# Two threads for the inverses, an urgent rank for what the column products lack, two-copy grams and recounted times in a hand-ordered encoder kernel

## The chip, the cores and the metric

The kernel runs on one core of a Trainium2 chip. The metric is the device time of one execution in microseconds. Inside the core, TensorE (PE) multiplies matrices into PSUM, VectorE (DVE) and ScalarE (ACT) do elementwise work and bring results out of PSUM, GpSimd (POOL) and SyncE (SP) mostly issue DMAs. Each engine works through its own instructions strictly in order and waits at semaphores for the others.

## The reference

Two requests of 512 tokens with 1024 features pass the same two layers. Layer 0 is RWKV-7 time mixing in both directions, layer 1 a neighbourhood attention on a grid of 8 x 64 tokens.

```python
def _wkv7_scan(r, decay, k, v, a, b, reverse):
    def step(s, inp):
        r_t, w_t, k_t, v_t, a_t, b_t = inp
        sa = jnp.einsum('bhvk,bhk->bhv', s, a_t)
        s = s * w_t[:, :, None, :] + sa[..., None] * b_t[:, :, None, :] + v_t[..., None] * k_t[:, :, None, :]
        return s, jnp.einsum('bhvk,bhk->bhv', s, r_t)
...
    for d in range(2):
        w_log = -jax.nn.softplus(-(w0[d] + jnp.tanh(xw @ w1[d]) @ w2[d]).astype(f32)) - 0.5
        decay = heads(jnp.exp(-jnp.exp(w_log)))
        a = heads(jax.nn.sigmoid((a0[d] + (xa @ a1[d]) @ a2[d]).astype(f32)))
        k_d = k * (1.0 + (a - 1.0) * k_a_h)
        ys.append(_wkv7_scan(r, decay, k_d, v, -kk, kk * a, reverse=(d == 1)))
```

Around this stand the large products with weights of 1024 columns each (`w_r`, `w_k`, `w_v`, `w_z`, `w_o`; then `w_in` with 4096 columns and `w_ao`), all in float32.

## The kernel before

**Stages.** The first stage (`prelude`) normalises the inputs and makes the first products. The second, `scan_phase`, holds the whole recurrence of both requests and, between its pieces, the large products that do not hang on it. The third, `rest`, holds the attention and the last products. A large product of float32 is made of three matmuls on rounded halves (high by high, high by low, low by high), so each weight tile must first be split: ACT writes the high half `whi` (line 782), DVE the low half `wlo` (line 784). The input tiles are split in the same way into pairs of `act` tiles (lines 808 and 810).

**The scan.** Tokens are cut into 8 chunks of 64. The 16 heads go in pairs of pairs, so that 2 requests x 4 give 8 *pairs*, each with 8 *steps*: 64 steps in a row. `prep` (twice for each pair) builds the scaled keys and queries (`ab`), and `gram` multiplies them into 32 x 32 blocks on PE (line 1012); ACT brings these from PSUM into `Gd` and `Go` (lines 1018 and 1019). `inverse` inverts the unit lower triangles: it transposes `Gd` into `N` on DVE (line 1048), makes 30 rank-1 updates there (lines 1055 and 1057, the *elimination*), writes the result transposed as `NA` and `MT` (lines 1065 and 1070), and then joins blocks of 32 into blocks of 64 by small matmuls and copies (lines 1074 to 1096, the *merges*). A step (`step`, `near`, `outer`, `factors`) solves with `MT` (matmuls of line 1250) and carries the state `S` on.

**What sets the order.** In `scan_phase` the order of PE, DVE and ACT is written by hand. Every piece of work is a `Thread`, a generator that yields before each instruction that has something to wait for. `weave` asks all threads whose gate is open and takes, among those that are ready by the counted time, the one with the lowest rank: steps 0, near and factors 0.5, outer 1, prep 1.5, the posts of columns (what follows a product) 2, operands 2.5, splits 3 where the stock is low and else 9, the inverse 5, the column products 9. The class `Clock` counts the times: it adds a cost for each instruction to the time of its engine. Only this counted time decides the order; on the chip the semaphores decide when a thing runs. Where nothing is ready for PE in the counted time, `weave` puts in a *filler* matmul (line 1681) that multiplies constants into an unused part of PSUM, as long as PE was busy for less than 70% of the last 3.4 us.

**Gates.** The inverse of pair n starts when its prep is through, when the inverse before it is through (it is one thread) and when the steps of the pair before the last are done. Prep n+1 starts when elimination n has taken `Gd`. Products of a group of columns (one input, such as `lv` of request 1) go in order: each column takes 8 input tiles k, and each k three matmuls (lines 863, 864, 865). Their gate asks for `w` (the split weight), `x` (the split input), a PSUM bank and, at k = 0, for the post of the column before the last.

Of the kernel before, what the change touches and what calls it, by code (L numbers as in the profile page):

```python
# [50 lines left out]
class Clock:  # L51
# [7 lines left out]
    def __init__(self, nc):  # L59
        self.nc = nc  # L60
        self.t = dict.fromkeys("PADGS", 0.0)
        self.made, self.used = {}, {}
        self.slots = {}
        self.slot = {}
        self.keep = set()
        self.dq = 0.0
        self.mode, self.tiles = None, {}
        self.seen = 0
        self.work = []
# [43 lines left out]
    def one(self, e, i):  # L113
# [51 lines left out]
        return 0.0 if e in "SG" and "dram" in str(type(outs[0].bass_ap.tensor)).lower() else done  # L165

    def matmul(self, i, ins, n, t):
        f32, tr = ins[0].dtype == F32, bool(i.is_transpose)
# [63 lines left out]
class Trunk:  # L232
# [21 lines left out]
    HACT = (3, 4)  # L254
    WARM = 300.0
    AHEADE = dict(S=3000.0, A=200.0, D=200.0)

# [85 lines left out]
    def consts(self):  # L343
# [17 lines left out]
        ts = nc.vector.tensor_scalar  # L361
        ts(dv[:, 0:32], v("w0", 32), 0.5, None, op0=ALU.mult)
        ts(dv[:, 32:40], v("ka", 8), 0.5, None, op0=ALU.mult)
        ts(dv[:, 40:48], v("ka", 8), -0.5, 1.0, op0=ALU.mult, op1=ALU.add)
# [303 lines left out]
    def column(self, s, kind, p, ps):  # L668
# [29 lines left out]
        if kind == "k":  # L698
# [15 lines left out]
            if p == NP - 1:  # L714
# [6 lines left out]
                yield "D"  # L721
                vt.tensor_scalar(rn, rn, 1e-12, None, op0=ALU.max)
                vt.reciprocal(rn, rn)
# [34 lines left out]
    def flow(self):  # L758
# [124 lines left out]

    def prep(self, s, p):
# [34 lines left out]
        vt.tensor_tensor(w2l, w2, w2h.bitcast(F32), op=ALU.subtract)  # L919
        yield "A", None, need(kk)  # L920
        km = b("km")
        act.mul(km, kk, -0.5)
        kps = []
        grams = None
        free, room = self.bank()
        for d in range(2):
            ths = []
            for q, bias in ((d, 8 * d + p), (2 + d, 16 + 8 * d + p)):
# [7 lines left out]
                th = b(f"th{q // 2}")  # L936
                act.activation(th, ps, AF.Tanh, scale=0.5, bias=self.dv[:, bias:bias + 1])
                ths.append(th)
                if len(ths) == 1:
                    u = b("u")  # L940
                    act.activation(u, th, AF.Identity, bias=self.one)
            if grams:
# [36 lines left out]
            yield "D", None, need(tha)  # L979
            vt.scalar_tensor_tensor(bb, tha, 1.0, kk, op0=ALU.add, op1=ALU.mult)  # L980
            yield "D", None, lambda c: max(need(e1)(c), ck)
            put(3, mul, c3(r), e1v)
            yield "D"
            put(2, mul, c3(km), e0v)
            yield "D", None, need(e2)
# [12 lines left out]
            def gram(ab=ab, d=d):  # L998
# [16 lines left out]
                yield "A", None, need(ps)  # L1015
                for par in range(2):
                    e = (par + d) % 2
                    act.copy(Gd[half(e), :, par::2, g], ps[half(e), :, :, 0:32])
                    act.copy(Go[half(e), :, par::2, g], ps[half(e), :, :, 32:64])

# [14 lines left out]

    def inverse(self, s, pb):

# [4 lines left out]
        NU = 32  # L1042
        free, room = self.bank()
        need = lambda *xs: lambda c, n=[x.tensor.name for x in xs]: c.at(n)
# [21 lines left out]
        MT = self.MTb[self.nM % 2]  # L1066
        self.nM += 1

        yield "D"
        vt.transpose(MT[:, :, 0, :].rearrange("p u i -> p i u"), N)  # L1070
        yield "A"
        for q in (1, 3):
# [123 lines left out]
    def step(self, q):  # L1196
# [49 lines left out]
        def solved():  # L1246
            for g in range(2):
                for h in range(2):
                    for r in range(2):
                        nc.tensor.matmul(  # L1250
                            u[half(1 - r), h, g], mt[half(r), h, st.i, g], Z[half(r), h, g], start=True, stop=True)
                        yield
# [443 lines left out]
    def scan_phase(self, mid):  # L1696
# [6 lines left out]
        self.MTb = [t(f"MT{j}", (P, 32, 2, 32)) for j in range(2)]  # L1703
        self.nM = 0

        self.cab = [t(f"cab{j}", (P, 17 * L)) for j in range(2)]
# [51 lines left out]
        def each(f):  # L1758
# [5 lines left out]
            Thread(lambda: 1, each(self.outer)),  # L1764
            Thread(lambda: 0, fetch()), Thread(lambda: 0, fetch_x()), *self.flow(), Thread(lambda: 5, inverse()), Thread(lambda: 1.5, preps()),
            Thread(lambda: 1.3 if did["finish"] == 3 else 4, finish()), Thread(lambda: 1.2, self.norm0(0))]
# [203 lines left out]
```

## Time and profile before

| quantity | value |
|---|---|
| median of 3 runs | 1650.11 us (1646.97 to 1652.83) |
| profiled execution | 1650.23 us |
| its span, first to last instruction | 1648.5 us |
| matmul passes of PE in the span | 18784 |
| filler matmuls (line 1681) | 80, of two passes each |

The span is what the profile's views divide. The first stage ends at about 150 us, the stage with the scan at about 1160 us. A float32 matmul whose operands are not rounded halves runs in two or four passes, so PE's counts in the profile are higher than in the program. A row of the groups view gives the line, engine and operation, the tiles (output before the arrow, inputs behind), the shape, the count, the union of busy time in us, the mean of one in ns and, behind the second bar, the idle time of the engine just before these instructions and what ended it.

### The profile page before, as it was taken

The page shows a single profiled execution, that of the slowest core. Times are in us where ns is not written, and L with a number is a line of the kernel's source. Part 1 is how long each engine was busy: PE and PEld are TensorE (multiplying, and loading weights), DVE is VectorE, ACT ScalarE, POOL GpSimd, SP SyncE. Part 2 cuts the span into 40 slices and gives each one's busy share as a digit, 9 for nine tenths or more (in the row PEclk, how much of TensorE's full clock was granted, in tenths as well). Part 3 has the DMA queues.
Part 4 walks back from the last instruction along what each step waited for, and adds up shares of the span by engine and source line. Part 5 has one row for each costly group of instructions (what it writes and reads, how often), then busy time and mean ns, then how long its engine had stood idle before and what let it go on. Part 6 is the DMA issues. An engine that isn't in the chain of part 4 may idle for free.

```text
span 1648.5 us, 46529 instructions
## 1 busy us (share of the span) xinstructions
PE 1545.7 (94%) x18784; PEld 1184.1 (72%) x18784; DVE 1218.2 (74%) x2713; ACT 1012.6 (61%) x2027; POOL 178.8 (11%) x336
## 2 busy tenths in 40 slices
PE   7988999889998999988989899999999999999998
PEld 5866767666676776766767667777777778777776
DVE  8986587678788797877898887855676585665564
ACT  6567676757765667667666655453667665465562
POOL 0001123201011011231010110000000002100000
PEclk9989999899999999999999999999999999999999
DMA  6447686766668578777687664564865346745553
GB/s 239 160 169 258 202 272 219 250 227 229 194 197 267 189 237 278 225 251 242 219 273 222 215 228 148 169 193 144 285 222 167 104 141 215 245 156 175 169 165 104
DMA packets 182008, 340.48 MB, mean 207 GB/s; under 512 B 25344, under 2 KB 58240, under 8 KB 181792
## 3 DMA queue, kind: packets, MB, share of 16 engines
q1 hardware_dynamic: 158144, 256.75, 48.4%
q0 software_dynamic: 23648, 80.76, 13.9%
q8 instruction: 148, 2.42, 0.6%
q14 instruction: 68, 0.56, 0.1%
HBM read 230.33 MB, written 107.09 MB: 205 GB/s over the span
## 4 chain that ended last, share of the span: by engine, by line
PE 45%; DVE 3%; ACT 3%; DMA 2%; issue 1%; DVEq 0%; POOL 0%; ACTq 0%; SPq 0%; POOLq 0%
PE pg L430 6%; PE pg L431 6%; PE pg L432 6%; PE pm L863 3%; PE pm L865 3%; PE pm L864 3%; PE sc L1489 2%; PE po L1522 2%; PE pt L1507 2%; PE pf L1151 1%; PE us L1250 1%; PE us L1270 1%; PE zy L1223 1%; PE pm L1476 1%; PE zy L1274 1%
## 5 line engine op out<-in xcount | busy, mean ns | idle before, releaser
L863 PE MATMUL pm<-act,whi 128*128 128x512 f32 x672 | 297.3, 442 | 2.9 <-ACT whi L782 2.2
L865 PE MATMUL pm<-act,wlo 128*128 128x512 f32 x672 | 268.7, 400 | 11.4 <-DVE wlo L784 10.7
L864 PE MATMUL pm<-act,whi 128*128 128x512 f32 x672 | 267.4, 398 | 6.9 <-DVE act L810 6.9
L865 PEld LDWEIGHTS pm<-act,wlo 128*128 128x128 f32 x672 | 127.9, 190 | 47.5 <-DVE wlo L784 18.4
L863 PEld LDWEIGHTS pm<-act,whi 128*128 128x128 f32 x672 | 127.7, 190 | 44.8 <-issue 12.9
L430 PE MATMUL pg<-act,whi 128*128 128x512 f32 x384 | 159.6, 416 | 0.0
L431 PE MATMUL pg<-act,whi 128*128 128x512 f32 x384 | 152.4, 397 | 0.0
L432 PE MATMUL pg<-act,wlo 128*128 128x512 f32 x384 | 152.1, 396 | 0.0
L864 PEld LDWEIGHTS pm<-act,whi 128*128 128x128 f32 x672 | 128.6, 191 | 31.9 <-DVE act L810 10.5
L379 ACT CAST whi<-raw 128x512 fp32r<-128x512 f32 x148 | 91.4, 617 | 85.5 <-PE pg L431 61.7
L784 DVE TENSOR_TENSOR wlo<-raw,whi 128x512 fp32r<-128x512 f32 x168 | 114.0, 683 | 39.8 <-ACT whi L782 39.5
L380 DVE TENSOR_TENSOR wlo<-raw,whi 128x512 fp32r<-128x512 f32 x148 | 101.3, 686 | 55.1 <-ACT whi L379 54.7
L782 ACT CAST whi<-raw 128x512 fp32r<-128x512 f32 x168 | 102.7, 618 | 43.2 <-PE pm L864 32.9
L432 PEld LDWEIGHTS pg<-act,wlo 128*128 128x128 f32 x384 | 72.1, 188 | 15.0 <-issue 0.3
L430 PEld LDWEIGHTS pg<-act,whi 128*128 128x128 f32 x384 | 72.3, 188 | 14.7 <-issue 3.3
L431 PEld LDWEIGHTS pg<-act,whi 128*128 128x128 f32 x384 | 72.5, 189 | 13.6 <-issue 2.5
L1057 DVE TENSOR_TENSOR N<-etmp,N 128x30 f32<-128x30 f32 (+14 forms) x240 | 78.7, 328 | 4.5
L1055 DVE TENSOR_TENSOR etmp<-N 128x30 f32<-128x30 f32 (+14 forms) x240 | 78.4, 327 | 4.2
L1151 PE MATMUL pf<-cab 64*64 64x128 f32 (+1 forms) x2048 | 68.5, 270 | 6.5 <-issue 6.5
L1500 DVE CUSTOM_DVE_ANT_0 sb<-sc,bias 128x256 f32<-128x256 f32 x128 | 49.6, 419 | 27.5 <-PE pt L1507 17.3
L1503 ACT ACTIVATE sb<-sb,mx 128x256 f32<-128x256 f32 x128 | 64.2, 503 | 9.3 <-DVE mx L1502 8.5
L1174 DVE TENSOR_TENSOR AK<-zy,cc 128x256 f32<-128x256 f32 x63 | 26.6, 422 | 56.4 <-PE zy L1129 53.0
(391 smaller groups left out, 3598.1 us busy)
## 6 DMA issues: line engine op xcount, KB each, us to landing
dab<-ab POOLq DMA_DIRECT2D x32, 1024.0 KB, 6.8
cab<-dab SPq DMA_DIRECT2D x64, 512.0 KB
raw<-in_w_in_dram SPq DMA_DIRECT2D x128, 256.0 KB
bias<-in_rpb_dram SPq DMA_DIRECT2D x32, 384.0 KB
raw<-in_w_z_dram SPq DMA_DIRECT2D x32, 256.0 KB
raw<-in_w_k_dram SPq DMA_DIRECT2D x32, 256.0 KB
raw<-in_w_r_dram SPq DMA_DIRECT2D x32, 256.0 KB
k<-dk SPq DMA_DIRECT2D x32, 256.0 KB
```

Of the source, the lines that this page charges most:

```text
L379: self.nc.scalar.copy(hi, src)
L380: (eng or self.nc.vector).tensor_tensor(lo, src, hi.bitcast(F32), op=ALU.subtract)
L430: nc.tensor.matmul(ps, hi, x[k][0], start=(k == 0), stop=False)
L431: nc.tensor.matmul(ps, hi, x[k][1], start=False, stop=False)
L432: self.mm = nc.tensor.matmul(ps, lo, x[k][0], start=False, stop=(k == KT - 1))
L782: nc.scalar.copy(hi, raw[h])
L784: nc.vector.tensor_tensor(lo, raw.pop(h), hi.bitcast(F32), op=ALU.subtract)
L863: nc.tensor.matmul(ps, hi[:, at], xh, start=(k == 0), stop=False)
L864: nc.tensor.matmul(ps, hi[:, at], xl, start=False, stop=False)
L865: nc.tensor.matmul(ps, lo[:, at], xh, start=False, stop=(k == KT - 1))
L1057: vt.tensor_tensor(N[:, q + 1:, :q], tv, N[:, q + 1:, :q], op=ALU.add)
L1151: end = nc.tensor.matmul(st.f[half(a), h, 0, d, g] if st.last else st.f[half(a), h, :, d, g], ab[half(h), d, g, 2 * e[d] + 1 - a], rt if s ...
```

## The change

Six things are altered.

1. `inverse` becomes two threads: `elimination` (rank 5) and `merges` (rank 2.4). Elimination n no longer waits for the merges of n-1 and for the steps of pair n-2 before it starts, only before it writes `NA` and `MT`.
2. The threads that supply products get the rank 1.2 while theirs is the first thing lacking within the next 8 input tiles of the column products: `short()` says whether that is a split weight, a split input or a post.
3. The grams leave PSUM in two ACT copies of 128 partitions instead of four of 64. The blocks then stand in another order, which the index of `mt` in `step` takes up.
4. The factor -0.5 that `km` (line 922) carried goes elsewhere: `rn` is scaled by the root of 2, `tha` is computed with a negative sign, and `dv` has other constants. The ACT instruction for `km` goes, and `kk` takes its place.
5. `u` is made by a copy with the number 1.0 instead of an activation with a tile of ones as bias.
6. `Clock` counts other times: 46 ns instead of 85 as ACT's start for an input in PSUM, 105 ns for each further operand of ACT, 112 ns where ACT changes its rows, 1283 ns for a change of its function table, 1.13 ns for each element of a DVE operation with a scalar and two tensors, and 104 and 48 ns on PE between matmuls on the full array and on parts of it.

The chains of work outside `scan_phase` are the same instructions.

```diff
@@ Clock.one
             if e == "A":
-                c = 85.0 + 0.85 * n
+                c = self.scalar(i, ins, outs, n)
...
-                c = 82.0 + 1.02 * n
+                c = 82.0 + (1.13 if getattr(i, "is_scalar_tensor_tensor", False) else 1.02) * n
@@ Clock
+    def scalar(self, i, ins, outs, n):
+        ap = outs[0].bass_ap
+        rows = (ap.offset // ap.ap[0][0] if ap.ap[0][0] else 0, ap.ap[0][1])
+        c = (46.0 if ins[0].bass_ap.tensor.name.startswith(self.BANKS) else 85.0) + 0.85 * n + 105.0 * (len(ins) - 1)
+        if rows != (0, 128) and rows != self.rows or self.rows[1] < 128 and rows[1] == 128:
+            c += 112.0
...
+            if self.table is not None and (f == "Sqrt") != self.table:
+                c += 1283.0
@@ Clock.matmul
+        full = ts == (128, 128)
+        if full and not tr and self.mode not in (None, ts):
+            c += 104.0
+        elif not full and self.mode == (128, 128):
+            t += 48.0
@@ Trunk
+    AHEADB, URGENT = 8, 1.2
@@ flow
+        def short():
+            for n in range(self.AHEADB):
+                b = did["k"] + n
+                c, k = divmod(b, KT)
+                if c >= len(cols):
+                    return None, n
+                if b // 4 not in w:
+                    return "w", n
+                if (cols[c][0], k) not in x:
+                    return "x", n
+                if k == 0 and c - 2 in self.post:
+                    return "post", n
+            return None, n
+        def rank(kind, usual):
+            def now():
+                what, n = short()
+                return self.URGENT if what == kind else usual()
+            return now
...
-            Thread(lambda: 0, loads()), Thread(lambda: 3 if few() else 9, splits()), Thread(lambda: 0, fetched()), Thread(lambda: 2.5, operands()),
+            Thread(lambda: 0, loads()), Thread(rank("w", lambda: 3 if few() else 9), splits()), Thread(lambda: 0, fetched()), Thread(rank("x", lambda: 2.5), operands()),
...
-            Thread(lambda: 9, products()), Thread(lambda: 2, posts(0)), Thread(lambda: 2, posts(1))]
+            Thread(lambda: 9, products()), *(Thread(rank("post", lambda: 2), posts(a)) for a in range(2))]
@@ prep
-        km = b("km")
-        act.mul(km, kk, -0.5)
...
-                    act.activation(u, th, AF.Identity, bias=self.one)
+                    act.activation(u, th, AF.Copy, bias=1.0)
...
-                for par in range(2):
-                    e = (par + d) % 2
-                    act.copy(Gd[half(e), :, par::2, g], ps[half(e), :, :, 0:32])
-                    act.copy(Go[half(e), :, par::2, g], ps[half(e), :, :, 32:64])
+                act.copy(Gd[:, :, 4 * d:4 * d + 4, g], ps[:, :, :, 0:32])
+                act.copy(Go[:, :, 4 * d:4 * d + 4, g], ps[:, :, :, 32:64])
@@ inverse
-    def inverse(self, s, pb):
+    def elimination(self, m, s, pb):
...
-        yield "D"
+        yield "D", lambda: self.did["inverse"] >= m and self.did["steps"] >= NCH * (m - 1)
         NA = f("NA", (P, NU, 32))
...
+    def merges(self, s, pb):
...
+        yield "A", None, need(MT)
@@ scan_phase
-                yield "D", lambda: did["preps"] > n and did["steps"] >= NCH * (n - 1)
-                yield from self.inverse(s, pb)
+                yield "D", lambda: did["preps"] > n
+                yield from self.elimination(n, s, pb)
+                did["eliminated"] += 1
+        def merges():
+            for n, (s, pb) in enumerate(self.todo):
+                yield "A", lambda: did["eliminated"] > n
+                yield from self.merges(s, pb)
                 did["inverse"] += 1
...
-... Thread(lambda: 5, inverse()), Thread(lambda: 1.5, preps()),
+... Thread(lambda: 5, inverse()), Thread(lambda: 2.4, merges()), Thread(lambda: 1.5, preps()),
```

Three places show how the order moves. The first is PE, early in the stage, in the first column of the second group (`pm` is a column's PSUM bank, `act` and `whi`, `wlo` the split input and weight, `zy<-cc` the filler). Before:

```order
L863 MATMUL pm_2236<-act_2280,whi_2247 128x512
L864 MATMUL pm_2236<-act_2279,whi_2247 128x512
L865 MATMUL pm_2236<-act_2280,wlo_2248 128x512
L1681 MATMUL zy_1593<-cc 128x256 x2
L863 MATMUL pm_2236<-act_2336,whi_2247 128x512
L864 MATMUL pm_2236<-act_2335,whi_2247 128x512
L865 MATMUL pm_2236<-act_2336,wlo_2248 128x512
L1681 MATMUL zy_1593<-cc 128x256 x4
```

The same column in the changed kernel:

```order
L887 MATMUL pm_2175<-act_2252,whi_2246 128x512
L888 MATMUL pm_2175<-act_2251,whi_2246 128x512
L889 MATMUL pm_2175<-act_2252,wlo_2247 128x512
L1729 MATMUL zy_1594<-cc 128x256 x3
L887 MATMUL pm_2175<-act_2280,whi_2246 128x512
L888 MATMUL pm_2175<-act_2279,whi_2246 128x512
L889 MATMUL pm_2175<-act_2280,wlo_2247 128x512
L1056 MATMUL pf_2297<-ab_2234 32x64 x32
```

Six fillers between three input tiles have become three. Over the whole stage 80 fillers in 38 rows have become 62 in 24 rows.

The second place is DVE in the second direction of the 14th of the 16 preps, where low halves of weights (`wlo`) stand beside the prep's writes into `ab`. Before:

```order
L950 SCALAR_TENSOR_TENSOR th_2166_11745<-cc,u_11747 128x512
L980 SCALAR_TENSOR_TENSOR pp_11824<-th_2169_11758,rb_11513 128x512
L977 TENSOR_TENSOR ab_11823<-r_11512,e_2175_11817 128x4x2x64
L977 TENSOR_TENSOR ab_11823<-km_11639,e_2175_11817 128x4x2x64
L977 TENSOR_TENSOR ab_11823<-pp_11824,u_11820 128x4x128
L784 TENSOR_TENSOR wlo_11740<-raw_11561,whi_11739 128x512
L784 TENSOR_TENSOR wlo_11843<-raw_11721,whi_11842 128x512
```

The same prep in the changed kernel:

```order
L808 TENSOR_TENSOR wlo_11783<-raw_11726,whi_11782 128x512
L834 TENSOR_TENSOR act_11840<-xr_10727,act_11841 128x512
L994 SCALAR_TENSOR_TENSOR th_2177_11774<-cc,u_11776 128x512
L1024 SCALAR_TENSOR_TENSOR pp_11866<-th_2188_11805,rb_11578 128x512
L1021 TENSOR_TENSOR ab_11865<-r_11577,e_2196_11859 128x4x2x64
L1021 TENSOR_TENSOR ab_11865<-rb_11578,e_2196_11859 128x4x2x64
L1431 TENSOR_TENSOR acc_11003<-tmp_11877,acc_11003 128x512
L834 TENSOR_TENSOR act_11853<-xr_10847,act_11854 128x512
L1021 TENSOR_TENSOR ab_11865<-pp_11866,u_11862 128x4x128
L808 TENSOR_TENSOR wlo_11845<-raw_11760,whi_11844 128x512
```

One of the two `wlo` now stands ahead of the prep's first DVE instruction, and halves of inputs (`act`) stand between its writes.

The third place is DVE where the elimination of the last pair begins, two rows behind the transpose into `MT` (line 1070) of the pair before it. Before:

```order
L820 TENSOR_TENSOR xr_12133<-xr_12133,vs_12135 128x512
L686 SCALAR_TENSOR_TENSOR tmp_12147<-tmp_12148,pm_12021 128x512
L784 TENSOR_TENSOR wlo_12103<-raw_12059,whi_12102 128x512
L818 SCALAR_TENSOR_TENSOR xr_12157<-xr_12157,cv,acc_10676 128x512
L820 TENSOR_TENSOR xr_12157<-xr_12157,act_12159 128x512
L784 TENSOR_TENSOR wlo_12231<-raw_12094,whi_12230 128x512
L784 TENSOR_TENSOR wlo_12268<-raw_12123,whi_12267 128x512
L818 SCALAR_TENSOR_TENSOR xr_12219<-xr_12219,cv,acc_10676 128x512
L820 TENSOR_TENSOR xr_12219<-xr_12219,act_12221 128x512
L686 SCALAR_TENSOR_TENSOR tmp_12314<-tmp_12315,pm_12149 128x512
L784 TENSOR_TENSOR wlo_12370<-raw_12206,whi_12369 128x512
L1048 STREAM_TRANSPOSE N_12381<-Gd_10554 128x1024
```

In the changed kernel, from the transpose into `MT` (there line 1109) on:

```order
L1109 STREAM_TRANSPOSE MT_417_1581<-N_10614 128x32x32
L842 SCALAR_TENSOR_TENSOR xr_12046<-xr_12046,cv,acc_11003 128x512
L844 TENSOR_TENSOR xr_12046<-xr_12046,vs_12048 128x512
L710 SCALAR_TENSOR_TENSOR tmp_12058<-tmp_12059,pm_11904 128x512
L1089 STREAM_TRANSPOSE N_12122<-Gd_10730 128x1024
```

The transpose that opens the elimination stood 13 rows behind that of `MT`, and stands 4 rows behind it now. Over the whole stage it stands at rows 279, 402, 571, 766, 949, 1109, 1301 and 1514 of DVE for the eight pairs before, and at 281, 419, 576, 766, 942, 1116, 1294 and 1514 now.

More of the change, by code (lines that the diff above doesn't have):

```diff
@@ L67, in __init__ @@
         self.mode, self.tiles = None, {}
+        self.rows, self.table = (0, 128), None
         self.seen = 0
@@ L165, in one @@
         return 0.0 if e in "SG" and "dram" in str(type(outs[0].bass_ap.tensor)).lower() else done
+    def scalar(self, i, ins, outs, n):
[4 more added lines that the diff above has]
+            c += 112.0
+        self.rows = rows
+        f = str(getattr(i, "func", "")).split(".")[-1]
+        f = f if f in ("Sqrt", "Tanh", "Exp") else None
+        if f:
+            if self.table is not None and (f == "Sqrt") != self.table:
+                c += 1283.0
+            self.table = f == "Sqrt"
+        return c
     def matmul(self, i, ins, n, t):
@@ L936, in prep @@
                 th = b(f"th{q // 2}")
-                act.activation(th, ps, AF.Tanh, scale=0.5, bias=self.dv[:, bias:bias + 1])
+                act.activation(th, ps, AF.Tanh, scale=-0.5 if q > 1 else 0.5, bias=self.dv[:, bias:bias + 1])
                 ths.append(th)
@@ L983, in prep @@
             yield "D"
-            put(2, mul, c3(km), e0v)
+            put(2, mul, c3(kk), e0v)
             yield "D", None, need(e2)
@@ L1061, in inverse @@
         vt.memset(N.rearrange("p i j -> p (i j)")[:, 0:1024:33], 1.0)
-        yield "D"
+        yield "D", lambda: self.did["inverse"] >= m and self.did["steps"] >= NCH * (m - 1)
         NA = f("NA", (P, NU, 32))
         vt.transpose(NA.rearrange("p u j -> p j u"), N.rearrange("p i j -> p j i"))
-        MT = self.MTb[self.nM % 2]
-        self.nM += 1
+        MT = self.MTb[m % 2]
         yield "D"
         vt.transpose(MT[:, :, 0, :].rearrange("p u i -> p i u"), N)
-        yield "A"
+        self.formed[s, pb] = wc, MT, NA, go
+    def merges(self, s, pb):
+        nc = self.nc
+        act, gps = nc.scalar, nc.gpsimd
+        wc, MT, NA, go = self.formed[s, pb]
+        free, room = self.bank()
+        need = lambda *xs: lambda c, n=[x.tensor.name for x in xs]: c.at(n)
+        yield "A", None, need(MT)
         for q in (1, 3):
@@ L1250, in solved @@
                         nc.tensor.matmul(
-                            u[half(1 - r), h, g], mt[half(r), h, st.i, g], Z[half(r), h, g], start=True, stop=True)
+                            u[half(1 - r), h, g], mt[half(r), h, (r ^ st.i % 2) * 4 + st.i // 2, g], Z[half(r), h, g], start=True, stop=True)
                         yield
@@ L1764, in scan_phase @@
             Thread(lambda: 1, each(self.outer)),
-            Thread(lambda: 0, fetch()), Thread(lambda: 0, fetch_x()), *self.flow(), Thread(lambda: 5, inverse()), Thread(lambda: 1.5, preps()),
+            Thread(lambda: 0, fetch()), Thread(lambda: 0, fetch_x()), *self.flow(), Thread(lambda: 5, inverse()), Thread(lambda: 2.4, merges()), Thread(lambda: 1.5, preps()),
             Thread(lambda: 1.3 if did["finish"] == 3 else 4, finish()), Thread(lambda: 1.2, self.norm0(0))]
```

12 lines of the change are left out of this document (5 added, 7 removed).

## The prediction

> **What bounds the kernel now.** I read the page first, for the shares of the engines and the 40 slices, then the busy times by stage.
>
> ```profile
> PE 1545.7 (94%) x18784; PEld 1184.1 (72%) x18784; DVE 1218.2 (74%) x2713; ACT 1012.6 (61%) x2027; POOL 178.8 (11%) x336
> PE   7988999889998999988989899999999999999998
> PEclk9989999899999999999999999999999999999999
> 0.00:150.00 150.00, 130.44 (x528) 98.12 (x528) 125.98 (x239) 103.14 (x173) 5.19 (x43) 0.96 0.59 208
> 150.00:1160.00 1010.00, 935.97 (x15507) 707.41 (x15506) 784.48 (x1512) 625.58 (x1217) 142.74 (x236) 0.98 0.68 220
> 1160.00:1648.50 488.50, 479.28 (x2752) 378.59 (x2750) 307.74 (x964) 283.84 (x639) 30.87 (x57) 1.00 0.54 178
> ```
>
> The last three rows give the stretch, its length, the busy time of PE, weight load, DVE, ACT and POOL, and then the granted clock. PE is the bound everywhere. The last stage is PE from end to end and its instructions are the same after the change, as are those of the first; I leave both at their times. The middle stage has 1010.0 - 936.0 = 74 us in which PE idles, and a mean clock of 0.98, which is about 0.02 x 1010 = 20 us of lost speed. This stage is where the change acts.
>
> Two chains run through it: the scan, step after step, and the column products, which have the lowest rank and fill PE. Which of them ends the stage is told by the first and last start of the solve (line 1250) and of the products (line 863).
>
> ```profile
> L1250 PE MATMUL us<-Z,MT x1024: 218/218/367, 310.4 to 1130.6; 64*64 64x64 f32 x171
> L863 PE MATMUL pm<-act,whi x672: 387/396/975, 154.0 to 1159.1; 128*128 128x512 f32 x168
> ```
>
> The scan is through at about 1130.6, the products at 1159.1. So the scan has 28.5 us to spare, and the end is set by the sum of PE's work, its fillers, its idle time and its clock. A shorter scan by itself earns nothing. Next, who ends PE's idle time in that stage, by groups and by waits.
>
> ```profile
> L863 PE MATMUL pm<-act,whi 128*128 128x512 f32 x672 | 297.3, 442 | 2.9 <-ACT whi L782 2.2 <-DVE bv L1343 0.6
> L865 PE MATMUL pm<-act,wlo 128*128 128x512 f32 x672 | 268.7, 400 | 11.4 <-DVE wlo L784 10.7 <-issue 0.5
> L864 PE MATMUL pm<-act,whi 128*128 128x512 f32 x672 | 267.4, 398 | 6.9 <-DVE act L810 6.9
> L1681 PE MATMUL zy<-cc 128*128 128x256 f32 x160 | 44.6, 403 | 4.3 <-DVE y L1291 2.8 <-ACT Z L1235 1.1 <-ACT y L1289 0.5
> PE pm L706 <- ACT tmp L702: 4.9, 2, 3.7
> ...
> PE pm L1086 <- ACT vs L743: 0.4, 1, 0.4
> PE pf L1151 <- issue: 6.5, 4, 3.0
> ```
>
> Products wait 10.7 + 2.2 = 12.9 us for split weights and 6.9 us for split inputs. The sixteen other rows of waits that ACT ends, of which the largest and the smallest are shown, sum to 24.4 us. Some 14 us, the largest part in the L1151 row, have no releaser; nothing in the change touches them. The rest is spread over DVE's other results.
>
> **The change, part by part.**
>
> *Fillers.* A timeline shows what one costs where it stands between products.
>
> ```profile
> 248.28 0.40 PE L865 MATMUL pm<-act,wlo 128*128 128x512 f32 x1
> 248.51 1.03 PE L1681 MATMUL zy<-cc 128*128 128x256 f32 x4
> 249.19 0.58 PE L863 MATMUL pm<-act,whi 128*128 128x512 f32 x1
> ```
>
> Two fillers (four passes) hold PE from 248.51 to 249.19, 0.34 us each. By the group row it is 44.6 / 80 = 0.56 us each. The order has 18 fewer, as the first of the three places shows: 6.1 to 10.0 us. It is nothing if the operands behind them are as late as before and idle time takes their place. I take **6 us**, from the timeline, since that is start to start.
>
> *ACT's work.* The rows that go, and rows like those that come:
>
> ```profile
> L1018 ACT COPY Gd<-pf 64x256 f32<-64x256 f32 x64 | 23.5, 367 | 15.2 <-PE pf L1012 14.5
> L1019 ACT COPY Go<-pf 64x256 f32<-64x256 f32 x64 | 23.5, 367 | 0.0
> L1235 ACT COPY Z<-zy 128x256 f32<-128x256 f32 x64 | 23.7, 371 | 50.3 <-PE zy L1229 44.8 <-PE zy L1681 5.1
> L922 ACT ACTIVATE km<-rb 128x512 f32<-128x512 f32 x16 | 10.2, 635 | 5.7 <-DVE rb L915 5.6
> L941 ACT ACTIVATE u<-th,ones 128x512 f32<-128x512 f32 x32 | 23.1, 723 | 1.9 <-DVE ab L977 0.8
> L734 ACT COPY tmp<-tmp 128x512 f32<-128x512 f32 x16 | 9.9, 616 | 0.0
> L1328 ACT ACT_TABLE_LOAD x8 | 10.3, 1283 | 0.1
> ```
>
> Gram copies: 128 of 0.367 us become 64, each like the 128x256 copy of `Z` with 0.371 us, so 47.0 - 23.7 = 23.3 us less. `km`: 10.2 us less. `u`: 32 x (0.723 - 0.616) = 3.4 us less. The order has two more table loads, 2 x 1.283 = 2.6 us more. In all 34.3 us less of ACT's 625.6, or 5.5%. DVE's work is unchanged, as `kk` takes the place of `km` in the same operation.
>
> The Trainium skill ("ScalarE: Activation LUTs", What ACT_TABLE_LOAD costs) puts a switch at about 2.66 us, the load and a drain. By that the two extra loads would cost 5.3 us and ACT's saving would be 31.6 us; the row above shows 1.283 us for the load and 0.1 us of idle time before all eight, so the trace shows no drain of that size there.
>
> ACT has 384 us of idle time in the stage, so its saving does not come off the end one for one; it comes off only where PE waits for ACT, the 24.4 us. The bounds are nothing (each copy keeps its place behind something else) and 24.4. The counted times speak for a part: with pointer operands, row changes and table loads now counted, PE's order should hold fewer matmuls that are written before ACT can have served them. I take a third, **8 us**; 5.5% less work would by itself give 1.3, and I know no row nearer.
>
> *Urgent splits and inputs.* The trace shows what a late `wlo` does at the second of the three places.
>
> ```profile
> 829.81 1.13 ACT L1371 COPY tmp<-pm 128x512 f32<-128x512 f32 x1
> 830.73 0.63 ACT L782 CAST whi<-raw 128x512 fp32r<-128x512 f32 x1
> 831.52 0.68 DVE L977 TENSOR_TENSOR ab<-pp,u 128x512 f32<-128x512 f32 x1
> 832.12 1.29 DVE L784 TENSOR_TENSOR wlo<-raw,whi 128x512 fp32r<-128x512 f32 x2
> 832.86 0.50 PE L865 MATMUL pm<-act,wlo 128*128 128x512 f32 x1 [2.56 <-DVE wlo L784]
> ```
>
> PE stands for 2.56 us because `wlo` is queued behind three writes into `ab`, 0.6 us apart. With the urgent rank a split is written ahead of the prep. Counting tile numbers in the order, 29 of 168 splits were written less than two input tiles ahead of their first product, and 22 are now; the first 18 are tight in both. So 7/29 of 12.9 us, **3 us**; the bounds are nothing and 12.9. For the inputs the order is no clear witness, since more of them now stand close to their use; bounds -2 (a few more of the late ones) and 6.9, and I take **2 us**.
>
> The urgent rank of 1.2 is above prep's 1.5, so preps come later, and behind them elimination and steps. The 28.5 us by which the scan ends early hides this; without that cover each us of it would count.
>
> *Two threads for the inverse.* In the trace the next elimination opens when the merges end:
>
> ```profile
> 407.05 2.11 ACT L1074 COPY MT<-MT 32x1024 f32<-32x1024 f32 x2 [0.24 <-DVE MT L1070]
> 420.13 1.17 ACT L1096 COPY MT<-pm 32x512 f32<-32x512 f32 x2
> 420.87 1.97 DVE L1048 STREAM_TRANSPOSE N<-Gd 128x1024 f32<-128x1024 f32 x1
> ```
>
> From `MT` at 407.05 to the copies at 420.13 the merges take 14 us, and only then `N` is begun at 420.87. That wait goes at places such as the third one. But over the whole stage the elimination opens at almost the same rows of DVE, for it now waits for its prep; and the scan is not what ends the stage. I cost it at **nothing**; the bound on the other side is in the rivals.
>
> *The clock.* After idle time PE runs at half speed for a while:
>
> ```profile
> 300.95 0.85 PE L1012 MATMUL pf<-ab 64*32 64x64 f32 x64 [2.17 <-DVE ab L977]
> 303.28 2.07 PE L1088 MATMUL pm<-MT,NA 32*32 32x32 f32 x64 [0.90 <-ACT MT L1096]
> 306.75 1.12 PE L740 MATMUL pm<-cc,tmp 128*128 128x128 f32 x4 [1.40 <-ACT vs L743]
> 306.00:309.50 3.50, 2.75 (x9) 0.50 1.03 386
> ```
>
> Three waits of 2.17, 0.90 and 1.40 us lead to a clock of 0.50. If idle time and fillers fall by the 19 us above, of 74 + 80 x 0.34 = 101, the 20 us of lost speed should fall in proportion: **4 us**. Fewer fillers could also raise it; bounds -5 and 9.
>
> The Trainium skill ("TensorE: Matmul & The Clock Gate", HAM oscillation — how this bites in real kernels) says that only idle gaps over about 3.4 us bring the clock down. By that next to nothing here should throttle, since only one wait of PE in the stage is over 3.0 us (3.7, in the L706 row, where the stage begins); the fillers would be idle work and this term about zero. The trace disagrees: it shows 0.50 behind three waits of under 2.2 us each.
>
> The sum is 6 + 8 + 3 + 2 + 4 = 23 us. The profiled execution took 1650.2 us (span 1648.5 and 1.7 around it), within 0.2 us of the median of the three runs, so the forecast is 1650.2 - 23 = **1627 us**.
>
> **The rivals.**
>
> *More goes than I take.* If counted times now fit and nothing that is late stays late, the upper bounds sum to 10 + 24.4 + 12.9 + 6.9 + 9 = 63 us, 1587 us. For it speaks that the waits are many and small, as a wrong count would leave them. Against it, fillers still stand in a cluster of 14 between inputs of the group that begins after the fourth pair, so inputs are still late there.
>
> *The waits only change places.* DVE has 784 of 1010 us, and its work is unchanged; what is put first there makes something else late. The fillers that go leave idle time, ACT's saving falls into ACT's idle time. That gives 1650 us, within 5.
>
> *Slower: the scan becomes the bound.* An urgent split (0.63 us on ACT, 0.69 on DVE) or a copy of the merges can stand ahead of `Z`, `X`, `AK` or `S` of a step, whose thread has rank 0 but cannot pass what is already written. If one DVE split came into each of the 64 steps, the scan would grow by 64 x 0.69 = 44 us, 28.5 of them hidden, and the stage by 16: 1666 us. It decides from 28.5 / 64 = 0.45 us for each step on. Against it, the order has 52 of the 672 products' input tiles behind the last solve, and had 36 before: the scan ends earlier among PE's work, not later.
>
> That the change does not do what it says holds for the elimination, as shown, and is in the sum at nothing.
>
> **How the numbers follow.** Forecast, 0.50, itself spread over 1612 to 1642; more goes, 0.17; change of places, 0.20; slower, 0.13. A measurement of this kernel tells about 0.3% from no change, that is 5 us. Faster by more: the first two and a little of the third, 0.70; within: most of the third, 0.17; slower: 0.13. The range reaches halfway into the second and over the third, **1597 to 1656 us**, and leaves out the deepest gains and most of the slower case.
>
> **What would show it.** In the changed profile PE's idle time between 150 us and the last product should be about 60 us instead of 74, with `wlo` and `whi` under 10 us and ACT's rows near 16; the stage should end near 1137; ACT's busy time there should be 34 us lower; the scan should end at least 30 us ahead of the products. I am wrong if idle time stays at 74 with other names, if the clock falls below 0.98, or if the last solve comes within 10 us of the last product.

## The result and the profile after

| | median us (runs) | ratio to before, 95% interval |
|---|---|---|
| before | 1648.84 (6) | |
| changed | 1637.25 (6) | 0.9919, 0.9898 to 0.9940 |
| forecast | 1627, range 1597 to 1656 | 0.986 |
| profiled execution of the changed kernel | 1627.3 | |

The changed kernel is faster by 0.8%, or 11.6 us by the medians. The forecast had the sign and the range right, and twice the gain. The profiled execution, from which the views below come, is the fastest of its six; it shows the whole 23 us of the forecast (1650.2 to 1627.3), so a reader has to keep two differences apart: what the order did in the profiled execution, and what the median execution gets of it. One execution of e8 below (2083.75 us at a granted clock of 0.654) fell into a slower state and is left out of its numbers.

First the page of the changed kernel, then its busy times by stage (columns as before), then the solve and the products by their first and last start.

```profile
PE 1533.3 (94%) x18748; PEld 1178.7 (73%) x18748; DVE 1218.4 (75%) x2714; ACT 983.7 (61%) x1949; POOL 179.2 (11%) x336
0.00:150.00 150.00, 130.82 (x529) 98.38 (x530) 127.37 (x242) 104.41 (x175) 5.20 (x43) 0.95 0.60 208
150.00:1137.00 987.00, 923.19 (x15477) 702.57 (x15476) 785.07 (x1529) 597.98 (x1145) 143.01 (x236) 0.98 0.70 228
1137.00:1625.50 488.50, 479.32 (x2745) 377.73 (x2743) 305.93 (x945) 281.31 (x630) 30.96 (x57) 1.00 0.53 172
L1298 PE MATMUL us<-Z,MT x1024: 218/218/366, 300.5 to 1096.4; 64*64 64x64 f32 x171
L887 PE MATMUL pm<-act,whi x672: 387/395/799, 153.7 to 1136.2; 128*128 128x512 f32 x168
```

The last stage is 488.5 us as it was, so all of the difference lies in the stage with the scan, which ends at 1136.2 instead of 1159.1. PE idles 987.0 - 923.2 = 64 us there, 10 less than before. ACT is busy 598 us instead of 626, 28 us less where 34 were to be seen. The scan is through 40 us ahead of the products, and was 29 ahead.

PE's groups in that stage, and the waits that ended most of its idle time (us in total, times, longest):

```profile
L887 PE MATMUL pm<-act,whi 128*128 128x512 f32 x672 | 294.6, 438 | 2.7 <-ACT act L832 1.0 <-ACT NA L1141 1.0 <-ACT whi L806 0.5
L888 PE MATMUL pm<-act,whi 128*128 128x512 f32 x672 | 268.0, 399 | 7.7 <-DVE act L834 6.8 <-issue 0.6 <-DVE N L1102 0.2
L889 PE MATMUL pm<-act,wlo 128*128 128x512 f32 x672 | 267.3, 398 | 6.6 <-DVE wlo L808 6.6
L1729 PE MATMUL zy<-cc 128*128 128x256 f32 x124 | 36.2, 430 | 0.0
PE pm L1136 <- issue: 6.0, 3, 4.7
PE pf L1199 <- issue: 5.9, 3, 2.8
PE zy L1177 <- issue: 5.6, 3, 2.1
PE pf L1056 <- issue: 4.0, 3, 2.8
PE pm L730 <- ACT tmp L726: 1.7, 2, 1.5
```

Split weights are waited for 6.6 + 0.5 = 7.1 us instead of 12.9, split inputs 6.8 + 1.0 = 7.8 instead of 6.9. The other rows that ACT ends sum to 13.4 us. The prediction's 24.4 us for them hold one wait that is over before the stage begins:

```profile
149.04 1.87 PE L706 MATMUL pm<-tmp,cc 128*2 128x512 f32 x2 [3.71 <-ACT tmp L702]
```

The changed kernel has the same wait (3.73 us) just outside its window. So 13.4 us stand beside 24.4 - 3.7 = 20.7, a fall of 7 us. Idle time without a releaser is 24 us instead of 14.

The ACT groups that took the place of the grams' four copies and of `u`, and the opening of the elimination of the third pair, seen on DVE and ACT:

```profile
L1060 ACT COPY Gd<-pf 128x256 f32<-128x256 f32 x32 | 11.9, 371 | 17.2 <-PE pf L1056 16.9
L1061 ACT COPY Go<-pf 128x256 f32<-128x256 f32 x32 | 12.1, 379 | 0.0
L985 ACT ACTIVATE u<-th 128x512 f32<-128x512 f32 x32 | 20.3, 634 | 1.0
407.10 1.94 DVE L1109 STREAM_TRANSPOSE MT<-N 128x1024 f32<-128x1024 f32 x1
409.50 1.93 DVE L1089 STREAM_TRANSPOSE N<-Gd 128x1024 f32<-128x1024 f32 x1
424.74 1.18 ACT L1144 COPY MT<-pm 32x512 f32<-32x512 f32 x2 [2.03 <-PE pm L1136]
```

A copy of 128 partitions takes 0.371 or 0.379 us where one of 64 took 0.367. `N` is begun at 409.50, 15 us ahead of the last copy of the merges, where before it had to follow that copy.

### The profile page after: what moved, and what is told of

It reads as the page before. It is cut to its first block, busy times and chain, and to the rows that moved or that the text cites. A ratio compares the mean times of both kernels' runs of the same rounds, so it can differ in the third digit from the quotient of the medians.

```text
span 1625.5 us, 46341 instructions
## 1 busy us (share of the span) xinstructions
PE 1533.3 (94%) x18748; PEld 1178.7 (73%) x18748; DVE 1218.4 (75%) x2714; ACT 983.7 (61%) x1949; POOL 179.2 (11%) x336
## 4 chain that ended last, share of the span: by engine, by line
PE 70%; DVE 11%; DMA 7%; issue 5%; ACT 5%; SPq 1%; DVEq 0%; POOL 0%; ACTq 0%; POOLq 0%
PE pm L887 8%; PE pg L454 7%; PE pg L455 6%; PE pg L456 6%; PE pm L888 6%; PE pm L889 6%; PE pf L1199 3%; DMA dab<-ab 2%; PE sc L1537 2%; PE po L1570 2%; PE us L1318 2%; PE pt L1555 2%; PE zy L1271 2%; PE us L1298 2%; DVE ab L1021 1%
## 5 line engine op out<-in xcount | busy, mean ns | idle before, releaser
L1310 ACT COPY X<-us 64x256 f32<-64x256 f32 x128 | 47.1, 368 | 33.5 <-PE zy L1177 31.7
```

## The experiments

Twelve kernels were timed, each beside the kernel before on the same chip: e1 to e8 on one, e9 to e12 on another, so they are compared by their ratios. In the table the stage runs from 150 us to the start of the last matmul of the column products, in each kernel's own profile; "rest" is the stage less PE's idle time, less 0.56 us for each filler (the group row of the kernel before, 44.6 / 80), less half of the time at half speed (the part of the stage in which the trace's record of the granted clock has 0.5). The last column is the time from the start of the last solve to that of the last product.

| kernel | ratio (95%) | stage | idle | fillers | half speed | rest | products end after last solve |
|---|---|---|---|---|---|---|---|
| before | 1 | 1009.6 | 74.0 | 80 | 49.9 | 866 | 29 |
| changed | 0.9919 (0.9898 to 0.9940) | 986.6 | 63.8 | 62 | 44.0 | 866 | 40 |
| e1 changed again | 0.9923 (0.9898 to 0.9948) | 989.5 | 64.1 | 62 | 48.1 | 867 | 40 |
| e2 ScalarE's work back | 0.9937 (0.9913 to 0.9961) | 994.5 | 65.5 | 62 | 49.7 | 869 | 40 |
| e3 no fillers | 0.9903 (0.9876 to 0.9930) | 992.0 | 81.7 | 0 | 85.3 | 868 | 40 |
| e4 before, ScalarE's work cut | 0.9955 (0.9934 to 0.9976) | 997.7 | 71.9 | 80 | 29.6 | 866 | 29 |
| e5 before, new counts | 1.0031 (1.0008 to 1.0054) | 1014.8 | 72.1 | 100 | 51.2 | 861 | 52 |
| e6 before, urgent rank | 1.0066 (1.0041 to 1.0090) | 1022.0 | 67.3 | 106 | 67.0 | 862 | 19 |
| e7 before, two threads | 0.9999 (0.9977 to 1.0021) | 1014.9 | 80.9 | 67 | 59.4 | 867 | 52 |
| e8 changed, a trifle moved | 0.9925 (0.9899 to 0.9951) | 993.6 | 70.3 | 60 | 54.7 | 862 | 37 |
| e9 changed, not urgent | 1.0030 (1.0009 to 1.0052) | 1008.7 | 78.7 | 72 | 47.8 | 866 | 51 |
| e10 changed, one thread | 1.0011 (0.9992 to 1.0030) | 1005.0 | 69.3 | 83 | 41.4 | 869 | 17 |
| e11 changed, old counts | 1.0144 (1.0119 to 1.0170) | 1030.4 | 84.1 | 87 | 61.4 | 867 | 23 |
| e12 before, a trifle moved | 1.0024 (1.0006 to 1.0043) | 1010.2 | 72.8 | 77 | 54.7 | 867 | 24 |

The rest is 861 to 869 us in all fourteen profiles, though their stages differ by 44 us. So a stage is PE's fixed work of some 866 us, and beyond it idle time, fillers and half speed: those three say where a difference lies, to within these 8 us. The stages are of single executions, the ratios of several.

**e1, the changed kernel again.** No edit.

> The changed kernel once more, for a second profile of it. The first profile took 1627.3 us, 10 us below the median of its six runs, at the highest granted clock of the six (0.981). Theory A (the first profile was lucky with the clock): the time is again near 1637, and this profile has 50 us or more at half speed in the stage with the scan where the first had 41, with idle time of TensorE near 64 us again. Theory B (what differs is waits): half speed stays near 41 us and the idle time of TensorE in the stage is 70 us or more. In both, the idle time that no instruction released stays above 20 us, where the kernel before had 14.

It took 1638.56 us in the median. Neither theory holds: the profiled execution was again the fastest of its six (1630.1), with half speed at 48 us, between the two, and idle time at 64. (The expectation's 41 us for the first profile leave out the slow slot that is open when the stage begins; the table's 44 hold it.) Idle time without a releaser was 24 us again. How far the spread between executions goes with the clock is shown by the runs of the kernel before, in the last section.

**e2, ScalarE's work put back in the same order.** The turns that the planner took were written down and are replayed here, so every engine has the changed kernel's order.

```diff
+                if d == 0 and q == 0:
+                    act.mul(b("km"), kk, -0.5)
...
-                    act.activation(u, th, AF.Copy, bias=1.0)
+                    act.activation(u, th, AF.Identity, bias=self.one)
...
-                act.copy(Gd[:, :, 4 * d:4 * d + 4, g], ps[:, :, :, 0:32])
-                act.copy(Go[:, :, 4 * d:4 * d + 4, g], ps[:, :, :, 32:64])
+                for e in range(2):
+                    act.copy(Gd[half(e), :, 4 * d:4 * d + 4, g], ps[half(e), :, :, 0:32])
+                    act.copy(Go[half(e), :, 4 * d:4 * d + 4, g], ps[half(e), :, :, 32:64])
```

> The changed kernel in its exact order of all engines, with ScalarE's work put back: four gram copies of 64 partitions instead of two, u with a tile of ones as bias, and km computed (and read by nobody). About 37 us more of ScalarE. The theory that ScalarE's work carries a good part of the gain (8 us in the prediction's sum): 6 to 12 us slower than the changed kernel, so 1643 to 1649. The rival, that the order alone made the gain and ScalarE's copies fall into its idle time: within 3 us of the changed kernel.

1638.83 us, 0.3 us above e1 by the medians and 1.7 by the means, with some 4 us of uncertainty. `km` is computed here but read by nobody, so ACT's time is put back, not the wait for `km`. The row of its stage shows ACT with the work back, 631 us instead of 598:

```profile
150.00:1144.50 994.50, 928.99 (x15476) 703.72 (x15476) 786.38 (x1530) 631.19 (x1226) 143.03 (x236) 0.97 0.70 226
```

33 us more of ACT cost PE 1.4 to 1.7 us of idle time against the two profiles of the changed kernel. In this order ACT's copies lie in its idle time; the rival holds.

**e3, the fillers left out, same order.** The turns of the planner that are fillers are dropped.

> The changed kernel in its exact order, without its 62 fillers. By the price of 0.34 us for each filler that stands between ready products: up to 62 x 0.34 = 21 us faster than the changed kernel, 1616. The rival, that a filler stands where TensorE would idle anyway and keeps its clock up: as many microseconds of new idle time, and more time at half speed, so no faster than the changed kernel or up to 15 us slower, 1637 to 1652.

1632.45 us, 6 us below the changed kernel by the medians, with intervals that overlap. The 62 fillers stood for 62 x 0.56 = 35 us, and without them there are 18 us more of idle time and 41 us more at half speed, which cost 20. So half of a filler is idle time with a name, and what the fillers keep of the clock (0.978 on average in e1, 0.969 here) is about what they take. By the profiles the stage is 3 to 5 us longer without them, by the medians the time is shorter: it is not told from no change. It shows too that 0.56 is the right price and 0.34 too low: with 0.56 the rest comes out at 868 here and 866 in the changed kernel, with 0.34 at 868 and 880.

**e4, ScalarE's work cut in the order of before.** The reverse of e2, with `step`'s index and the constants that go with it.

> The kernel before in its exact order, with ScalarE's work cut as in the change (two gram copies, no km, u without the bias tile). The theory that ScalarE's work counts: 6 to 12 us faster than before, about 1640, with the sixteen ScalarE rows of TensorE's waits falling from 24 us to about 15. The rival, that only the new order brings those waits down: within 3 us of before, and the rows stay near 24.

1642.71 us, 0.45% faster. The size is the theory's, the way is not: the rows of waits for ScalarE fell by 2 us only. What fell is the time at half speed, 30 us instead of 50, and the mean granted clock of its eight runs is 0.9834 against 0.9789 over 35 runs of before. Why this order, with shorter copies, is throttled less often is not settled.

**e5, e6, e7: one part of the change alone on the kernel before.** The new count of times; the urgent rank; the two threads. The order is written anew in each.

> The kernel before, and of the change only the new count of times; the order is written anew by it. The theory of the prediction (counted times that fit take matmuls away that are written too early): TensorE's waits for ScalarE and for split operands fall together by 10 us or more, and the time is 6 to 12 us shorter, though the order now has 100 fillers. The rival, that counts alone only turn surprise waits into foreseen ones, filled with fillers: the waits fall, the fillers grow by 20 x 0.34 = 7 us, and the time is within 4 us of before.

> The kernel before, and of the change only the urgent rank of what the next column products lack. My step took 5 us for it: waits for wlo, whi and act fall from 20 us to about 15, and the time is about 5 us shorter. The rival, that preps come later and the scan is the bound: the last solve comes within 10 us of the last product and the time is longer by more than 3 us; the order has 106 fillers.

> The kernel before, and of the change only the inverse in two threads. My step costed this at nothing: within 4 us of before. The rival, that it is the carrier of the gain, since the next elimination fills VectorE's idle time during the merges (the order has 67 fillers where before has 80): 8 us or more faster, about 1640, and the last solve earlier than 1130.6 us by 15 us or more.

The counts alone cost 0.3%, the urgent rank alone 0.7%, the threads alone give nothing. With the counts alone PE's waits for split operands (21 us beside 20) and for ACT's other results (23 beside 21) do not fall, so the theory of e5 fails there; whether the order is worse or merely another cannot be told at 0.3% (see e12).

The urgent rank does what its name says: waits for split operands fall from 20 us to 14, as expected. The rows of the kernel with the urgent rank, with 0.6 us for `whi` and 0.3 us more for `act` besides:

```profile
PE pm L864 <- ACT act L809: 4.1, 3, 2.5
PE pm L866 <- DVE wlo L785: 3.5, 3, 2.5
PE pm L865 <- DVE act L811: 2.7, 7, 0.6
PE pm L864 <- ACT act L833: 2.6, 3, 1.8
```

But look at what ends most of PE's idle time in that kernel:

```profile
PE pm L958 <- DVE w2l L943: 6.5, 3, 5.9
PE pm L957 <- ACT w2h L941: 5.0, 1, 5.0
PE us L1294 <- ACT X L1286: 4.2, 7, 1.3
```

The halves of `w2`, which open a prep, are now waited for 11.5 us; before the change they made 0.2 us on PE:

```profile
PE pm L934 <- DVE w2l L919: 0.2, 1, 0.2
```

The prep has been pushed back, the last solve comes at 1152.7 instead of 1130.6, and 26 more fillers fill what is not there to do. The rival's mechanism is there, though not its end: the products still end 19 us after the scan, not within 10. With the threads alone the last solve comes at 1113.2, 17 us earlier than before, and 13 fillers go, but idle time rises by 7 us and half speed by 10, and in the profile nothing is left (its execution took 1654.3 us, 4.5 above the median of its runs).

**e8, e12: a trifle moved.** `EPS`, how far ahead a thing counts as ready, from 60.0 to 61.0 ns in the changed kernel and in the kernel before.

> The changed kernel with one number of the planner moved by a trifle (a thing counts as ready 61 ns ahead instead of 60), so that the order falls a little otherwise for no reason. If the gain hangs on reasons: within 4 us of the changed kernel. If orders that are equally good on paper differ by as much as the change earned: more than 6 us from the changed kernel, either way.

> The kernel before with the same trifle in the planner (61 ns instead of 60), for the spread that an order has for no reason. If single parts of 5 us can be told from such a spread: within 3 us of before. If not: 5 us or more from before, and then the runs of single parts (0.3% and 0.7% slower, 0.4% faster) say little of their parts.

The changed kernel does not move (0.9925), the kernel before is 0.24% slower, between its two signs. So, by these two trials, an order can differ by some 4 us for no reason, and a single part of 0.3% (e5) is not told from that. The whole change of 0.8% and the 0.7% of e6 are.

The profile of e8 shows more. Its time is the changed kernel's, but PE's waits for ACT's results other than split operands sum to 21.9 us, as many as before the change (20.7) and not 13.4, and 17 us have no releaser instead of 24. So such a row of one profile moves by 8 us for no reason and is no measure of what a part earned. What the changed kernel, e1 and e8 share against the kernel before is fewer fillers (62, 62 and 60 instead of 80), less waiting for split weights (7.1, 6.8 and 7.4 us instead of 12.9) and less for DVE's other results, `w2l` aside (5.4, 4.9 and 6.6 us instead of 17.9).

**e9, e10, e11: the change without one part.** Without the urgent rank; with the inverse in one thread; with the old counts. The last two also keep the pause of the kernel before in `prep` until `kk` is ready by the counted time, at the place where `km` was made; the changed kernel has no such pause, and what it does is not separated.

> The changed kernel without the urgent rank. Theory now (the urgent rank alone cost 11 us since it holds the scan back, and pays only where the two threads give the scan its time back): without it the waits for split operands rise from 14 us to about 20, fillers to 72, and the time is 4 to 8 us longer than the changed kernel, about 1643. Rival (the urgent rank is a loss everywhere, and the rest of the change carries it): 5 us or more faster than the changed kernel, 1632 or less.

> The changed kernel with the inverse in one thread as before. Theory: the scan is held back by the urgent rank and not helped; the order has 83 fillers and only 16 input tiles of products behind the last solve where the changed kernel has 52; the last solve comes within 12 us of the last product and the time is 10 to 18 us longer than the changed kernel, 1648 to 1656. Rival (the prediction's step, that the two threads are worth nothing): within 4 us of the changed kernel.

> The changed kernel with the old count of times. Theory: with ScalarE counted short, matmuls are written too early again: waits for ScalarE and split operands 8 us higher than in the changed kernel, 87 fillers where it has 62 (8 us), the time 8 to 16 us longer, 1646 to 1654. Rival (the counts are worth nothing or cost as they did alone): the same as the changed kernel or up to 5 us faster.

Each is slower than the changed kernel by about the whole gain or more: by 1.1, 0.9 and 2.2 points of the ratio to before. The sizes of e9 and e11 are above what I expected. Without the urgent rank the idle time is 15 us higher, of which the split operands are 10 (25 us instead of 15), and there are 10 more fillers. With one thread there are 21 more fillers and the last solve comes at 1138.3 instead of 1096, though still 17 us ahead of the last product and not within the 12 that I expected. With the old counts idle time is 20 us higher, there are 25 more fillers, and half speed is 17 us longer. The waits of the last kernel:

```profile
PE pm L708 <- ACT tmp L704: 7.0, 2, 5.7
PE pm L866 <- DVE act L812: 6.2, 8, 1.8
PE zy L1156 <- issue: 5.8, 4, 2.1
PE us L1297 <- ACT X L1289: 5.4, 8, 1.3
```

They have many owners, ACT above all: its results other than split operands are waited for 24 us instead of 13. That matmuls are written before ACT can have served them is a guess, since e8 has 22 us of such waits with the new counts. The three planner parts earn together what none of them earns alone: as sums of single effects they would cost 0.96% (0.31 + 0.66 - 0.01) and with e4's 0.45% gain the whole would be 0.5% slower; it is 0.8% faster.

None of the twelve beats the changed kernel clearly; e3 comes nearest.

## Why the prediction was right, point by point

- **The bound and the frame were right.** The stage is PE's work and what lies beside it; the last stage did not move; the scan ended 40 us ahead, above the 30 that were to be seen. The table's rest of 861 to 869 us shows the frame in fourteen profiles. Of the signs of being wrong one came up, a clock below 0.98: the mean granted clock of the changed kernel's 12 runs is 0.9773, though the kernel before had 0.9789 already.
- **The sum was right for the profile by errors that cancel, which is luck.** Profile against profile it gives 23 us: 10 of idle time, 10 of fillers, 3 of half speed. Of the forecast's terms, ACT's waits fell by 7 (8 taken, as a third of 24.4 us of which 20.7 lay in the stage), fillers by 18 x 0.56 = 10 (6 taken; the price was from two fillers that stood between busy matmuls), splits by 6 (3 taken), the clock gave 3 (4 taken). Split inputs gave -1 (2 taken). Left out were 10 us more without a releaser, of which the prediction said that nothing in the change touches them, about 11 us less for DVE's other results (18 to 7), and 2 us more for DMAs. By e8 the shares of ACT and of the waits without a releaser are no more than those of one profile.
- **The median got half, and the step that failed is in good part the clock's.** I took its 4 us from the fall of idle time. Over the executions there is no such gain: the mean granted clock of the changed kernel's 12 runs is 0.9773, of 35 runs of before on the chip of e1 to e8 0.9789. At the same clock, by a line through each kernel's runs, the changed kernel is 14.6 us faster at 0.978. So of the 11 us by which the median falls short, about 7 are the clock (a loss of 3 for a gain of 4), and some 4 stay open. The line is a weak one: without the two profiled executions the other ten show no fall with the clock (correlation -0.14), and are 13.6 us below before's line at their mean clock. Both profiled executions were also fast for their clock, by about 4 us in the first; why is open.
- **The example for the clock was read in the wrong order.** The record of the clock has 0.50 from 302.3 to 312.5 us. Only the wait of 2.17 us stands ahead of that; in the 3.3 us from 298.9 to 302.2 PE was busy 1.25 us. The waits of 0.90 and 1.40 us lie inside the slow stretch and cannot have led to it. The stage's lost speed was also half of 49.9, so 25 us and not 20.
- **ACT's 8 us had the wrong cause.** The prediction gave ACT's smaller work and the counts together. e2 shows that the work is worth 0 to 2 us in the new order, with some 4 us of uncertainty, and in e4 less work in the old order took 2 us off these waits. So where they fell, the order did it; e8 shows that they need not fall for the gain to stand.
- **"Nothing" for the two threads was right alone (e7) and wrong in company (e10: 0.9%).** The step argued from the scan not being the bound. It left out that the urgent rank takes time from preps, as the prediction itself said, and that the threads give the scan its time back: with the urgent rank the last solve comes at 1138.3 with one thread and at 1096.4 with two. Why a later scan costs time that still ends 17 us ahead of the products is not shown; 12 of the 18 us by which the stage of e10 is longer are its 21 more fillers.
- **The urgent rank was costed as a gain of 5 us; alone it is a loss of 11.** The rival in which it holds back the scan was given 0.13 and is in part what e6 shows, without the two threads: the scan comes later, but through the preps (the 11.5 us for `w2`) and not through splits that stand ahead of a step, and it still does not end the stage.

## What to carry to other kernels

When a planner's ranks, its gates and its counted times are changed together, price them together: here each alone costs or gives nothing, and each left out loses about the whole gain or more. Keep one order and replay it to tell what less work on an engine is worth (e2, e4) from what a new order is worth. And split a stage into fixed work, idle time, fillers and half-speed time before explaining a difference; the part that is moved tells where to look. Move a trifle in the planner once: what a row of waits does then, it does for no reason.

## What the runs showed of the hardware that was not expected

**The spread goes with the granted clock.** Over 35 runs of the kernel before, times fall by 1.1 us for each 0.001 of mean clock (correlation -0.84), between 0.973 and 0.985; 29 more on another chip give 1.1 us and -0.85. Two profiles are not compared without that number beside them.

**PE stops inside a batch of small matmuls, and the instruction queue is fetching then.** In the changed kernel PE stands for 2.85 us with two matmul passes of a batch left, and nothing releases it:

```profile
457.73 1.05 PE L1199 MATMUL pf<-cab 64*64 64x128 f32 x29
461.63 0.38 PE L1199 MATMUL pf<-cab 64*64 64x128 f32 x2 [2.85 <-issue]
q8 instruction: 147, 2.41, 0.6%
```

The start times of that queue's packets (16384 bytes each) beside the three longest of these gaps:

```
PE idle 458.78 to 461.63   packet at 459.25
PE idle 728.99 to 733.68   packet at 731.38
PE idle 749.88 to 752.70   packet at 750.32
```

In e1 PE stands at 460.15 to 462.47, 732.71 to 736.29 and 753.11 to 754.29, at the same lines: the places belong to the order, not to chance. All waits without a releaser make 24 us of the changed kernel's 64 us of idle time, and 8 to 24 us in the fourteen profiles.

A packet that starts within a gap proves little, for 147 packets in 1625 us fall into a third of all stretches of 2.85 us. The end of the gap tells more. In the fourteen profiles, between 150 and 1140 us, PE has 157 waits of 0.4 us or more without a releaser, and 151 of them end 2.15 to 2.75 us after the start of a packet of that queue. Of the 598 waits of that length that have a releaser 36 do, 6%, and of moments taken at random 7%. So these waits end with the arrival of instructions, as far as timing can show it; no run here takes them away.
